# Grouped attention's projections run row by row beside the making of the modulated input; layer 1's last adaLN blocks beside its attention

## The chip, the cores and the metric

The kernel runs on one core of one Trainium2 chip. The metric is the device time of one execution in microseconds. The engines are called TensorE (PE in the rows; PEld is its weight load), the vector engine (DVE), the scalar engine (ACT), the Pool engine (POOL) and the sync engine (SP), whose queue issues most transfers.

## What is computed

Two layers of a hybrid backbone over 512 latent and 256 context tokens of width 1024, float32. Cut to what the change touches:

```python
for l in range(DEPTH):                                     # DEPTH = 2
    shift, scale, gate = split(silu(c) @ ada_w + ada_b, 3)  # adaLN; the context has its own vector
    pl = split_cols(modulate(x, shift, scale) @ in_w, IN_SPLITS)    # modulate: layer_norm(x) * (1 + scale) + shift
    ...
    q, k, v = gqa_project(pl[6], pl[7], pl[8], q_norm, k_norm, rope64)
    #   q: 4 heads of 64, k and v: 2 heads of 64; q and k: rms_norm, then rope (latent tokens only)
    oc = softmax_attention(q, k, v, GQA_SCALE)             # latent tokens read context and latent
    ...
    x = post_norm(ALPHA * x + gate * merge_branches(...), ln_g, ln_b)
```

The three other mixers (latent attention, RWKV-7, differential attention) and the merge follow the same input. In layer 1 the context's queries are not needed.

## The kernel before

**Tiles.** The 768 tokens are six tiles of 128 (0 and 1 context, 2 to 5 latent); the 1024 channels are eight blocks d of 128. Each float32 operand of a large product is split into a high and a low part, and three matmuls per tile and block are summed in PSUM (high by high, high by low, low by high). `w_split` (L280) loads a weight, copies the high part on the scalar engine (L292) and subtracts on the vector engine (L295).

**Start, layer 0** (`_run_layers`, L1525). The tokens are loaded and normalised. Then, for each of four adaLN blocks b, `ada` (L376) runs eight small float32 matmuls on c, which the trace counts as 16, with streamed weights (L391, `adaw`, twelve buffers), copies the row out (E, L396), turns it to columns (L399) and adds the bias (L403); after each block `make_xhat` (L454) is called for d = 2b and 2b+1. It transposes the six token tiles (L599, in `tok_T`), applies scale and shift while reading PSUM (L461 on the vector engine for context, L464 on the scalar engine for latent), and splits the result: for an even d on the vector engine (L478, L479), for an odd d on the scalar and Pool engines (L475, L476). PSUM has one pool A of eight one-bank buffers here.

**Projections of grouped attention.** The attention's pools are then opened, and `gq_proj` (L887) calls `m_stream` (L548): it loops over the eight channel blocks and, for each, over the token tiles, 144 matmuls of 256 columns in layer 0 (L570). Only after the last block it evicts Q tile by tile (L889), followed by the head norm (`head_rms`: squares L851, sums L852, reciprocal root L270 to L277), the scaling (L866, L867) and the rope (L590 to L593, with one multiplication on Pool, L592). `gkv_proj` (L870) does the same for K and V with 144 matmuls of 288 columns (L570), evictions L877 to L879. In layer 1 there are 96 and 144 matmuls, since Q is wanted for four tiles only.

**What sets the order.** The program is written as generators; the matmuls of other projections and of `ada` are `fill()`, advanced by rates `FILL` beside the attention's own steps (`beside`). A scheduler then puts the instructions of each engine in one fixed order. In layer 0, `fill()` also makes adaLN blocks 4 and 5 of layer 0 and blocks 0 to 3 of layer 1.

**Transition to layer 1** (L1662 on). The output projection, residual and post-norm run token by token (L1515, L1517, L432, L433), the second normalisation ends with L430. In a loop over d `make_xhat` runs for layer 1, with steps of `ada` for blocks 4 and 5 of layer 1 in between:

```python
more = K.ada(l + 1, ad, vec, xp, range(4, 6))
for _ in range(LEAD[0]):
    next(more)
for d in range(8):
    K.make_xhat(d, xn, ad, xp)
    for _ in range(LEAD[1]):
        next(more, None)
run(more)
```

## Time and profile before

| | |
|---|---|
| median of 3 runs | 2122.58 us (2116.28 to 2130.12) |
| the profiled execution, its own time | 2122.06 us |
| its span, first to last instruction | 2120.0 us |
| mean granted TensorE clock | 0.964 of full |
| busy: TensorE, its weight loads | 1932.8 us (91%), 1562.9 us (74%) |
| busy: vector, scalar, Pool engine | 1159.4 (55%), 816.2 (38%), 184.6 us (9%) |

The span is 2.06 us shorter than the execution's own time; the times in the rows count from the span's start. A granted clock of 1.00 is TensorE's full speed. In a timeline several instructions of one kind that follow each other stand in one row, with their count (x12) and the time from the first one's start to the last one's end; square brackets give the idle time ahead of it on its engine and what ended it. Layer 0's attention begins near 90 us, layer 1's near 1268 us.

### The profile page before, as it was taken

To read this page: it belongs to the slowest core of one execution; us is meant where nothing else is said; L and a number is where in the kernel's file an instruction comes from. 1 tells how busy PE (TensorE), PEld (TensorE's weight loads), DVE (VectorE), ACT (ScalarE), POOL (GpSimd) and SP (SyncE) were. 2 spreads that over 40 slices of the span, in tenths; PEclk is the share of its full clock that TensorE was granted. 3 is DMA by queue.
4 is the path that set the end of the run, shared out by engine and by line. 5 is a ranking of instruction groups with operands and counts; after the bars stand their busy time and mean duration, and the time that the engine had idled before them with its cause. 6 is when DMAs were issued, how large, how long until landed. Compare 5 with 4: busy or idle time off the path is not lost. (4 is left out here: it accounts for less than half of the span.)

```text
span 2120.0 us, 45780 instructions
## 1 busy us (share of the span) xinstructions
PE 1932.8 (91%) x19694; PEld 1562.9 (74%) x19694; DVE 1159.4 (55%) x2469; ACT 816.2 (38%) x1647; POOL 184.6 (9%) x283
## 2 busy tenths in 40 slices
...
GB/s 281 32 31 28 55 89 81 81 61 30 58 71 71 73 80 79 71 72 110 256 149 105 119 43 21 44 39 39 34 21 90 84 69 69 87 77 76 230 173 40
DMA packets 62322, 176.00 MB, mean 83 GB/s; under 512 B 7416, under 2 KB 12200, under 8 KB 62120
## 3 DMA queue, kind: packets, MB, share of 16 engines
...
q8 instruction: 155, 2.54, 0.5%
q14 instruction: 47, 0.39, 0.1%
...
## 5 line engine op out<-in xcount | busy, mean ns | idle before, releaser
L302 PE MATMUL ps<-xh,wx 128*128 128x384 f32 (+2 forms) x3096 | 690.5, 369 | 3.3 <-issue 1.9
L302 PEld LDWEIGHTS ps<-xh,wx 128*128 128x128 f32 x3096 | 535.1, 190 | 72.6 <-issue 16.0
L292 ACT ACTIVATE wx<-wx 128x1024 fp32r<-128x1024 f32 (+1 forms) x92 | 97.9, 1064 | 293.7 <-PE ps L302 224.4
L295 DVE TENSOR_TENSOR wx<-wx,wx 128x1024 fp32r<-128x1024 f32 (+1 forms) x92 | 113.4, 1232 | 129.4 <-ACT wx L292 126.5
L646 DVE TENSOR_REDUCE nmax<-ps 128x1 f32<-128x768 f32 (+1 forms) x160 | 134.7, 846 | 79.9 <-PE ps L643 78.6
L570 PE MATMUL ps<-wx,xh 128*128 128x256 f32 (+1 forms) x1200 | 156.1, 288 | 7.7 <-DVE mu L991 6.7
L570 PEld LDWEIGHTS ps<-wx,xh 128*128 128x128 f32 x1200 | 151.6, 191 | 10.6 <-ACT xc L475 6.8
L302 PE MATMUL ps<-xh,wb 128*128 128x384 f32 (+1 forms) x576 | 129.5, 375 | 26.5 <-DVE th L1473 17.9
L537 PE MATMUL ps<-wx,xh 128*128 128x256 f32 x960 | 141.3, 301 | 10.8 <-DVE oth L1407 5.8
L649 ACT ACTIVATE E<-ps,nmax 128x768 f32<-128x768 f32 (+1 forms) x160 | 130.1, 814 | 49.3 <-DVE nmax L646 44.7
L537 PEld LDWEIGHTS ps<-wx,xh 128*128 128x128 f32 x960 | 129.6, 203 | 18.5 <-DVE oth L1407 6.0
L643 PE MATMUL ps<-qk,qk 96*128 96x384 f32 (+3 forms) x504 | 131.2, 367 | 12.3 <-ACT E L649 11.8
L302 PEld LDWEIGHTS ps<-xh,wb 128*128 128x128 f32 x576 | 104.1, 195 | 48.4 <-DVE th L1473 15.5
L667 ACT ACTIVATE PH<-ps 128x512 f32<-128x512 f32 x156 | 91.7, 595 | 92.2 <-PE ps L665 89.4
L643 PEld LDWEIGHTS ps<-qk,qk 96*128 96x128 f32 (+1 forms) x504 | 82.6, 192 | 49.4 <-issue 22.6
L689 PE MATMUL ps<-PH,V 128*64 128x256 f32 x624 | 106.3, 414 | 3.2 <-ACT PH L667 2.8
L665 PE MATMUL ps<-cstalways,E 128*128 128x128 f32 x624 | 103.9, 288 | 5.1 <-DVE E L954 2.6
L1433 ACT ACTIVATE mth<-ps,hmb 128x384 f32<-128x384 f32 (+1 forms) x96 | 58.5, 610 | 118.5 <-PE ps L302 118.1
L665 PEld LDWEIGHTS ps<-cstalways,E 128*128 128x128 f32 x624 | 75.6, 146 | 26.5 <-issue 10.6
L625 DVE TENSOR_TENSOR qk<-ps,qk 32x256 fp32r<-32x256 f32 (+7 forms) x104 | 59.2, 574 | 36.9 <-ACT qk L624 34.7
L295 DVE TENSOR_TENSOR wx<-wf,wx 128x1024 fp32r<-128x1024 f32 (+2 forms) x34 | 41.1, 1210 | 59.8 <-PE ps L302 33.4
L624 ACT ACTIVATE qk<-ps 96x256 fp32r<-96x256 f32 (+3 forms) x104 | 51.2, 502 | 38.1 <-PE ps L599 37.5
...
## 6 DMA issues: line engine op xcount, KB each, us to landing
...
```

Source lines behind the costliest of these rows:

```text
L292: nc.scalar.activation(out=hi[:, :n], in_=raw[:, :n], func=AF.Copy)
L295: eng.tensor_tensor(out=lo[:, :n], in0=raw[:, :n], in1=hi[:, :n].bitcast(F32), op=ALU.subtract)
L302: self.nc.tensor.matmul(o, lhsT=w, rhs=x[:, s] if s is not None else x, start=first and p == 0, stop=last and p == 2)
L537: self.nc.tensor.matmul(ps[:, j * n:j * n + n], lhsT=self.xtok(x[k], s), rhs=w, start=k == 0 and p == 0 and j == 0, stop=k == 7 and p == 2 ...
L570: self.nc.tensor.matmul(ps, lhsT=self.xtok(x[k], s), rhs=w[:, c], start=k == 0 and p == 0 and head, stop=k == 7 and p == 2 and (tail or t ...
L625: nc.vector.tensor_tensor(out=lo[r, s], in0=ps[r], in1=hi[r, s].bitcast(F32), op=ALU.subtract)
L643: nc.tensor.matmul(o, lhsT=qt[:n, q], rhs=kt[:n, s], start=i == 0, stop=i == len(passes) - 1)
L646: nc.vector.tensor_reduce(out=nm, in_=v, axis=AX.X if ctx else AX.XY, op=ALU.max, negate=True)
L649: nc.scalar.activation(out=self.halves(e[:, :n], v), in_=v, func=AF.Exp, bias=nm, accum_out=den)
L665: nc.tensor.transpose(pt[:, c:c + 128], e[:, (k0 + k) * 128:(k0 + k) * 128 + 128], self.ident)
L667: nc.scalar.activation(out=hi, in_=pt, func=AF.Copy)
L689: nc.tensor.matmul(po[64 * (kk % 2):64 * (kk % 2) + 64, :n], lhsT=v2(kk), rhs=x[:, s], start=kk < 2, stop=kk >= nk - 2)
```

## The change

A generator `early_proj` takes over the first part of the projections of grouped attention. It opens six PSUM banks (pool G) at once: in layer 0 three hold Q for all six token tiles (two tiles a bank) and three hold K and V for three tiles; in layer 1 two hold Q for the four latent tiles and four hold K and V of four tiles. After each `make_xhat(d)` one row of the product, channel block d, is issued for all of these tiles: 27 matmuls in layer 0, 24 in layer 1. Weights are loaded for two rows at a time, Q's and KV's in one tile of 1088 columns (`wg`), split on the scalar and vector engines. The banks are evicted after the last row. The other tiles of K and V (three in layer 0, two in layer 1) follow in `m_stream`, which loads the K and V weights again. The pool for transposes and adaLN, A, has two banks beside the six; in layer 0's output projection too. The adaLN weights of the start get six buffers in place of twelve. Blocks 4 and 5 of layer 1's adaLN go from the transition to `fill()` of layer 1's attention, so both layers treat them alike. Line numbers after the change are higher by one up to L868 (L302 becomes L303), and L571 is the matmul of `m_stream`; L911 is the matmul of the rows.

```diff
--- before.py
+++ after.py
@@ -38,6 +38,7 @@
 QN = 256
 EB = 6
 QB = 8
+QSW, KSW = 384, 384
 GC = 2
 
 
@@ -866,29 +867,66 @@
         self.nc.vector.tensor_tensor(out=xv, in0=xv, in1=r, op=ALU.mult)
         eng.tensor_tensor(out=xv, in0=xv, in1=self.bc[g].unsqueeze(1).unsqueeze(1).to_broadcast(shape), op=ALU.mult)
 
+    def gqa_tiles(self):
+        self.gq = self.t(self.ap, [128, NT, QSW], "Qs", bufs=1)[:, :, :256]
+        self.gk = self.t(self.ap, [128, NT, KSW], "Ks", bufs=1)[:, :, :128]
+        self.gv = self.t(self.ap, [128, NT, 4, 64], "V2", bufs=1)[:, :, :2]
+        self.kr = self.t(self.ap, [128, NT, 32], "kr", bufs=1)
+
+    def use_q(self, t, o):
+        self.nc.scalar.activation(out=self.gq[:, t], in_=o, func=AF.Copy)
+
+    def use_kv(self, t, o):
+        self.nc.vector.tensor_copy(self.kr[:, t], o[:, 256:])
+        self.nc.scalar.activation(out=self.gk[:, t], in_=o[:, :128], func=AF.Copy)
+        self.nc.scalar.activation(out=self.gv[:, t], in_=o[:, 128:256].rearrange("p (h d) -> p h d", h=2), func=AF.Copy)
+
+    def early_proj(self, l, qt, pool):
+
+
+        nc = self.nc
+        self.gqa_tiles()
+        jobs = []
+        for i in range(0, len(qt), 2):
+            ps = self.P("G")
+            jobs += [(qt[i + j], ps[:, j * 256:j * 256 + 256], "gq", 0, 256, j == 0, j == 1, self.use_q) for j in range(2)]
+        early = range(6 - len(qt) // 2)
+        self.late = range(len(early), NT)
+        for t in early:
+            jobs.append((t, self.P("G")[:, :288], "gkv", 512, 288, True, True, self.use_kv))
+        off = _offsets()[0]
+        for k0 in range(0, 8, 2):
+            raw, hi, lo = (self.t(pool, [128, 1088], f"wg{x}", F32R if x else F32, bufs=2) for x in range(3))
+            for n, c, w in (("gq", 0, 256), ("gkv", 512, 288)):
+                o = off[n][0] + k0 * w
+                nc.sync.dma_start(out=raw[:, c:c + 2 * w], in_=self.a["inw"][l][:, o:o + 2 * w])
+            nc.scalar.activation(out=hi, in_=raw, func=AF.Copy)
+            nc.vector.tensor_tensor(out=lo, in0=raw, in1=hi.bitcast(F32), op=ALU.subtract)
+            for k in range(k0, k0 + 2):
+                for t, ps, n, c, w, head, tail, use in jobs:
+                    s = slice(t * 128, t * 128 + 128)
+                    c = slice(c + (k - k0) * w, c + (k - k0) * w + w)
+                    for p, (x, ww) in enumerate(((self.xh, hi), (self.xh, lo), (self.xl, hi))):
+
+                        nc.tensor.matmul(ps, lhsT=self.xtok(x[k], s), rhs=ww[:, c], start=k == 0 and p == 0 and head,
+                                         stop=k == 7 and p == 2 and tail)
+                yield
+        for t, ps, n, c, w, head, tail, use in jobs:
+            use(t, ps)
+
     def gkv_proj(self, l):
-        nc = self.nc
         toks = range(NT)
-        Ks = self.t(self.ap, [128, NT, 384], "Ks", bufs=1)[:, :, :128]
-        V2 = self.t(self.ap, [128, NT, 4, 64], "V2", bufs=1)[:, :, :2]
-        kr = self.t(self.ap, [128, NT, 32], "kr", bufs=1)
-
-        def use(t, o):
-            nc.vector.tensor_copy(kr[:, t], o[:, 256:])
-            nc.scalar.activation(out=Ks[:, t], in_=o[:, :128], func=AF.Copy)
-            nc.scalar.activation(out=V2[:, t], in_=o[:, 128:256].rearrange("p (h d) -> p h d", h=2), func=AF.Copy)
-        self.m_stream(l, "gkv", toks, use)
+        self.m_stream(l, "gkv", self.late, self.use_kv)
+        Ks = self.gk
         r = self.head_rms(Ks, 2, toks, 1.0, 1e-6)
-        self.scale_heads(Ks, 2, toks, r, "gkn", nc.vector)
+        self.scale_heads(Ks, 2, toks, r, "gkn", self.nc.vector)
         self.rope(Ks[:, NCT:].rearrange("p t (h d) -> p t h d", h=2), 2, 64)
-        return Ks, V2, kr
+        return Ks, self.gv, self.kr
 
     def gq_proj(self, l, qt):
-        nc = self.nc
-        Qs = self.t(self.ap, [128, NT, 384], "Qs", bufs=1)[:, :, :256]
-        self.m_stream(l, "gq", qt, lambda t, o: nc.scalar.activation(out=Qs[:, t], in_=o, func=AF.Copy))
+        Qs = self.gq
         r = self.head_rms(Qs, 4, qt, GQA_SCALE, 1e-6)
-        self.scale_heads(Qs, 4, qt, r, "gqn", nc.vector)
+        self.scale_heads(Qs, 4, qt, r, "gqn", self.nc.vector)
         self.rope(Qs[:, NCT:].rearrange("p t (h d) -> p t h d", h=4), 4, 64)
         return Qs
 
@@ -1528,7 +1566,9 @@
     ad = K.new_ada()
     xst, xct = ExitStack(), ExitStack()
     K.xp, K.xc = xst.enter_context(mk("xh0", 16)), None
-    with mk("xn0") as xp0, K.psum(A=(1, 8)):
+    ast = ExitStack()
+    K.ap = ast.enter_context(mk("at0"))
+    with mk("xn0") as xp0, K.psum(A=(1, 2), G=(1, 6)):
         xn = []
         for t in range(NT):
             x = K.t(xp0, [128, 1024], "xn", bufs=NT)
@@ -1537,9 +1577,13 @@
         K.normalise_all(xn, xp0)
         K.xh, K.xl = [], []
         for b in range(4):
-            run(K.ada(0, ad, vec, xp0, [b], (xp0, 12)))
+            run(K.ada(0, ad, vec, xp0, [b], (xp0, 6)))
+            if b == 0:
+                proj = K.early_proj(0, range(NT), xp0)
             for d in (2 * b, 2 * b + 1):
                 K.make_xhat(d, xn, ad, xp0)
+                next(proj)
+        run(proj)
     for l in range(DEPTH):
         last = l == DEPTH - 1
         qt = range(NCT, NT) if last else range(NT)
@@ -1553,8 +1597,7 @@
 
         def fill():
             yield from K.rwkv_inputs(l)
-            if l == 0:
-                yield from K.ada(0, ad, vec, K.ep, range(4, 6))
+            yield from K.ada(l, ad, vec, K.ep, range(4, 6))
             if not last:
                 nxt["vec"] = K.layer_vectors(l + 1)
                 nxt["ad"] = K.new_ada()
@@ -1564,8 +1607,7 @@
                     yield
                 yield from K.out_gate(l, i, O[i], qt, K.ep)
         ready = set()
-        with mk(f"qk{l}", QB) as K.qp, mk(f"ep{l}", EB) as K.ep, mk(f"at{l}") as K.ap, \
-                mk(f"wf{l}") as K.fp, K.psum(S=(2, 2), T=(1, 2), F=(1, 1), O=(1, 1)):
+        with mk(f"qk{l}", QB) as K.qp, mk(f"ep{l}", EB) as K.ep, mk(f"wf{l}") as K.fp, K.psum(S=(2, 2), T=(1, 2), F=(1, 1), O=(1, 1)):
             K.ps["A"] = K.ps["T"]
             K.load_group("rope", K.ap)
             K.load_rows(l, _BC_ATTN, K.ap)
@@ -1594,6 +1636,7 @@
         if only == "attn":
             return
         K.fp = None
+        ast.close()
         left = ExitStack()
         xct.close()
         K.rp = mkr(f"rw{l}")
@@ -1659,10 +1702,11 @@
                     next(tail)
                 gates_ = {s: K.gate_rows(ad, s) for s in ((1,) if last else (0, 1))}
                 run(tail)
-        with K.psum(A=(1, 8)):
+        with K.psum(**(dict(A=(1, 8)) if last else dict(A=(1, 2), G=(1, 6)))):
             ys = K.out_operands(y, len(qt) * 128)
             if not last:
-                ws = [K.out_weights(l, 0, mkr(f"ow0{l}"))]
+                ost = ExitStack()
+                ws = [K.out_weights(l, 0, ost.enter_context(tc.tile_pool(name=f"ow0{l}", bufs=1, side="right")))]
             left.close()
             xn = dict(h)
 
@@ -1678,20 +1722,20 @@
                 ws.append(K.out_weights(l, 1, owp))
                 K.out_proj(ys, ws, qt, gates_, h, first, second)
             if not last:
+                ost.close()
                 vec, ad = nxt["vec"], nxt["ad"]
                 K.xh, K.xl = [], []
                 xst.close()
                 K.xp = xst.enter_context(mk(f"xh{l + 1}", 16))
                 K.xc = xct.enter_context(mk(f"xc{l + 1}", 16)) if l + 1 == DEPTH - 1 else None
+                ast = ExitStack()
+                K.ap = ast.enter_context(mk(f"at{l + 1}"))
                 with mk(f"xn{l}") as xp:
-                    more = K.ada(l + 1, ad, vec, xp, range(4, 6))
-                    for _ in range(LEAD[0]):
-                        next(more)
+                    proj = K.early_proj(l + 1, range(NCT, NT), xp)
                     for d in range(8):
                         K.make_xhat(d, xn, ad, xp)
-                        for _ in range(LEAD[1]):
-                            next(more, None)
-                    run(more)
+                        next(proj)
+                    run(proj)
         right.close()
     xst.close()
 
```

How this moves instructions, at three places. First TensorE in layer 0, at the border of two adaLN blocks. Names: `xn` are normalised tokens (transposes), `adaw` adaLN weights, `wg` the new weights, `xh` the modulated input. Before:

```order
L599 MATMUL ps_298<-cstalways_113,xn_143 128x128
L391 MATMUL ps_308<-adaw_309,cs_118 32x512 x2
L391 MATMUL ps_308<-adaw_313,cs_118 32x512 x2
L391 MATMUL ps_308<-adaw_317,cs_118 32x512 x2
L391 MATMUL ps_308<-adaw_321,cs_118 32x512 x2
L399 MATMUL ps_327<-sum_46_121,E_325 128x2 x4
L599 MATMUL ps_337<-cstalways_113,xn_133 128x128
L599 MATMUL ps_337<-cstalways_113,xn_135 128x128
```

and now:

```order
L600 MATMUL ps_409<-cstalways_113,xn_145 128x128
L600 MATMUL ps_409<-cstalways_113,xn_147 128x128
L600 MATMUL ps_409<-cstalways_113,xn_149 128x128
L392 MATMUL ps_446<-adaw_447,cs_118 32x512 x2
L392 MATMUL ps_446<-adaw_451,cs_118 32x512 x2
L392 MATMUL ps_446<-adaw_455,cs_118 32x512
L911 MATMUL ps_245<-wg_107_371,xh_366 128x256
L911 MATMUL ps_245<-wg_108_372,xh_366 128x256
L911 MATMUL ps_246<-wg_107_371,xh_366 128x256
L911 MATMUL ps_245<-wg_107_371,xh_367 128x256
```

The last transposes of a pair of channel blocks (L599, now L600) were followed by the next adaLN block and its column turn (L399); now five of the eight adaLN matmuls stand there, then the 54 matmuls of two rows, and only then the other three.

Second, the vector engine in layer 0 between the modulated input's last channels and Q's head norm (`hm` holds the square sums, `kr` the part of K for latent attention, `mu` and what follows it are small constants). Before:

```order
L478 CAST xh_405<-mt_394 128x768
L479 TENSOR_TENSOR xh_406<-mt_394,xh_405 128x768
L295 TENSOR_TENSOR wx_540<-wx_538,wx_539 128x1024
L295 TENSOR_TENSOR wx_665<-wx_663,wx_664 128x1152
L852 TENSOR_REDUCE hm_622<-E_623 128x12
L852 TENSOR_REDUCE hm_622<-E_626 128x12
L295 TENSOR_TENSOR wx_743<-wx_741,wx_742 128x1152
L853 TENSOR_SCALAR hm_622<-hm_622 128x24
L270 TENSOR_SCALAR hr_630<-hm_622 128x24
```

and now:

```order
L880 COPY kr_244<-ps_248 128x32
L880 COPY kr_244<-ps_249 128x32
L880 COPY kr_244<-ps_250 128x32
L1029 TENSOR_TENSOR mu_184_909<-pp_111 128x8
L1032 TENSOR_SCALAR hw_185_912<-pp_111 128x4
L1033 TENSOR_SCALAR ha_186_913<-pp_111 128x4
L1030 TENSOR_SCALAR mu_184_909<-mu_184_909 128x8
L1034 TENSOR_SCALAR c_188_915<-pp_111 128x2
L1040 TENSOR_SCALAR nkk_922<-pp_111 128x2
L1035 TENSOR_SCALAR c_187_914<-c_188_915 128x2
L853 TENSOR_REDUCE hm_730<-E_731 128x12
L853 TENSOR_REDUCE hm_730<-E_734 128x12
```

Before, weight splits for the running projections (L295) stood ahead of Q's sums (L852); now the copies of the three early K and V tiles (L880) stand there, which come after the last row, and Q's sums (L853) behind them. In both kernels K's sums follow Q's whole chain.

Third, TensorE in the transition to layer 1 (`h` are normalised tokens). Before, at the end of the modulated input:

```order
L599 MATMUL ps_13176<-cstalways_113,h_1849_11549 128x128
L599 MATMUL ps_13176<-cstalways_113,h_1850_11551 128x128
L599 MATMUL ps_13176<-cstalways_113,h_1851_11553 128x128
L599 MATMUL ps_13176<-cstalways_113,h_1852_11555 128x128
L399 MATMUL ps_13200<-sum_46_121,E_13198 128x2 x4
L570 MATMUL ps_13245<-wx_13247,xh_13026 128x256
L570 MATMUL ps_13245<-wx_13248,xh_13026 128x256
L570 MATMUL ps_13245<-wx_13247,xh_13028 128x256
L570 MATMUL ps_13245<-wx_13247,xh_13026 128x256
```

and now, at its start:

```order
L600 MATMUL ps_13035<-cstalways_113,h_1860_11577 128x128
L600 MATMUL ps_13095<-cstalways_113,h_1860_11577 128x128
L600 MATMUL ps_13134<-cstalways_113,h_1855_11567 128x128
L600 MATMUL ps_13134<-cstalways_113,h_1856_11569 128x128
L911 MATMUL ps_13053<-wg_2164_13060,xh_13042 128x256
L911 MATMUL ps_13053<-wg_2165_13061,xh_13042 128x256
L911 MATMUL ps_13054<-wg_2164_13060,xh_13042 128x256
L911 MATMUL ps_13054<-wg_2165_13061,xh_13042 128x256
L911 MATMUL ps_13055<-wg_2164_13060,xc_13041 128x288
L911 MATMUL ps_13055<-wg_2165_13061,xc_13041 128x288
```

The first projection matmul stood behind the last of the 48 transposes and both adaLN turns (L399); the first row now follows the transposes of the first channel blocks.

## Rows read from the trace of the kernel before

**Rows 1.** Busy time by stretches: us, busy of each engine, granted clock, DMA share.

```profile
28.00:40.00 12.00, 10.48 (x89) 7.13 (x90) 6.87 (x21) 6.83 (x11) 3.62 (x2) 1.00 0.60 235
40.00:60.00 20.00, 19.02 (x156) 18.56 (x155) 5.81 (x7) 5.85 (x11) 2.63 (x1) 1.00 0.40 130
60.00:80.00 20.00, 20.00 (x154) 20.00 (x154) 16.05 (x33) 7.65 (x17) 2.72 (x5) 1.00 0.11 34
80.00:100.00 20.00, 11.75 (x62) 9.05 (x61) 12.88 (x33) 9.29 (x24) 1.52 (x2) 0.74 0.09 27
1200.00:1210.00 10.00, 4.65 (x24) 1.49 (x25) 7.91 (x39) 4.25 (x5) 0.00 (x0) 0.72 0.39 140
1210.00:1220.00 10.00, 5.76 (x29) 4.66 (x29) 9.18 (x13) 7.89 (x13) 5.76 (x8) 0.67 0.59 194
1220.00:1230.00 10.00, 6.87 (x38) 6.90 (x39) 5.20 (x17) 1.71 (x3) 1.97 (x2) 0.59 0.06 19
1520.00:1540.00 20.00, 16.57 (x110) 12.11 (x110) 19.23 (x34) 15.09 (x32) 0.00 (x0) 1.00 0.05 8
```

**Rows 2.** Timeline, layer 0, one adaLN block: start, us, engine, line, operation, [idle, releaser].

```profile
33.08 1.05 PE L399 MATMUL ps<-sum,E 128*128 128x2 f32 x8 [0.72 <-ACT E L396]
...
33.99 1.51 PE L599 MATMUL ps<-cstalways,xn 128*128 128x128 f32 x12
...
35.43 1.92 PE L391 MATMUL ps<-adaw,cs 128*32 128x512 f32 x16
...
36.34 0.96 DVE L479 TENSOR_TENSOR xh<-mt,xh 128x768 fp32r<-128x768 f32 x1
...
38.07 1.05 PE L399 MATMUL ps<-sum,E 128*128 128x2 f32 x8 [0.72 <-ACT E L396]
```

**Rows 3.** Timeline, layer 0, projections of Q, K and V.

```profile
41.43 36.99 PE L570 MATMUL ps<-wx,xh 128*128 128x256 f32 x288 [0.93 <-ACT mt L464]
...
58.60 1.77 ACT L889 ACTIVATE Qs<-ps 128x256 f32<-128x256 f32 x6 [2.77 <-PE ps L570]
...
66.97 1.76 DVE L866 TENSOR_TENSOR Qs<-Qs,hr 128x1536 f32<-128x1536 f32 x1
...
70.44 1.22 DVE L295 TENSOR_TENSOR wx<-wf,wx 128x1024 fp32r<-128x1024 f32 x1
...
74.29 2.37 DVE L593 TENSOR_TENSOR Qs<-Qs,E 128x512 f32<-128x512 f32 x2 [1.30 <-POOL Qs L592]
```

**Rows 4.** Timeline, layer 0, end of K's chain and the first attention matmuls.

```profile
81.36 0.55 DVE L852 TENSOR_REDUCE hm<-E 128x6 f32<-128x384 f32 x1 [1.16 <-ACT E L851]
...
87.92 1.26 DVE L593 TENSOR_TENSOR Ks<-Ks,E 128x256 f32<-128x256 f32 x2 [0.62 <-POOL Ks L592]
...
90.84 0.69 PE L599 MATMUL ps<-cstalways,E 128*128 128x128 f32 x2 [7.38 <-DVE qk L625]
```

**Rows 5.** Timeline, transition to layer 1.

```profile
1209.83 1.33 PE L599 MATMUL ps<-cstalways,h 128*128 128x128 f32 x5 [2.25 <-ACT h L430]
...
1211.90 0.42 DVE L478 CAST xh<-mt 128x512 fp32r<-128x512 f32 x1
...
1213.32 1.27 POOL L476 TENSOR_TENSOR xh<-mt,xh 128x512 fp32r<-128x512 f32 x1 [13.54 <-ACT xh L475]
1213.54 1.33 DVE L478 CAST xh<-mt 128x512 fp32r<-128x512 f32 x1
...
1223.13 14.01 PE L570 MATMUL ps<-wx,xh 128*128 128x256 f32 x96 [6.70 <-DVE mu L991]
```

**Rows 6.** Timeline, layer 1, head chains and the first attention matmuls.

```profile
1244.21 1.22 DVE L866 TENSOR_TENSOR Qs<-Qs,hr 128x1024 f32<-128x1024 f32 x1
...
1265.97 1.26 DVE L593 TENSOR_TENSOR Ks<-Ks,E 128x256 f32<-128x256 f32 x2 [0.61 <-POOL Ks L592]
...
1268.16 0.69 PE L599 MATMUL ps<-cstalways,E 128*128 128x128 f32 x2 [7.54 <-ACT E L614]
```

## Prediction

> **What bounds the kernel now.** I read the busy time by stretches first, at the two places that the change touches. In layer 0, TensorE is busy 19.02 and 20.00 us of 20 in two stretches and then 11.75 [rows 1]: there is almost nothing to fill while the modulated input is made and projected, and the hole comes after. In the transition to layer 1 the three stretches from 1200 to 1230 have 4.65, 5.76 and 6.87 of 10 busy, 12.7 us idle, at granted clocks of 0.72, 0.67 and 0.59 [rows 1]; a full clock is the 2.4 GHz level, and at the lower level, 1.2 GHz, a matmul takes twice as long. The timelines say what the holes are. In layer 0, one block of the input takes 4.99 us from one L399 to the next (33.08 to 38.07), with 0.72 us idle each, waiting for the copy E [rows 2]. With three of these and the 0.93 us ahead of the projection [rows 3] that is 3.1 us. The 288 projection matmuls then run without a gap, 36.99 us [rows 3]: the 144 for Q until the first Q eviction at 58.60 (17.17 us, 0.119 each), the other 144, for K and V, in 19.8 us (0.1375 each). The hole of 7.38 us ends at 90.84 [rows 4]. It is the vector engine's chain on K: square sums, reciprocal root, scaling and rope, last L593 at 87.92 + 1.26 = 89.18. In layer 1 the same hole is 7.54 us, behind an L593 that ends at 1267.23 [rows 6], and the projection before it starts 6.70 us late [rows 5]. What ends that wait is put down to a small vector instruction; going by the pools it is the turnover of PSUM, since all transposed tiles must have been read first.
>
> So what sets the time at both places is when the last Ks is ready. I work out how far that moves.
>
> **Layer 0.** Q's evictions, 58.60 on, and its chain, up to the L593 at 74.29 + 2.37 = 76.66, now run under the K and V matmuls [rows 3]. In the changed kernel all six banks close with the last row, so no Q can be evicted before the last row, and the vector engine's order has Q's chain wholly ahead of K's. Let R be the end of the last row. From the first Q eviction to L866 before were 8.37 us (58.60 to 66.97), and from there to the end of L593 9.69 [rows 3]; so Q is ready at R + 18.1. K's chain follows: two reductions (0.55 each), the weight split between them (1.22, as at 70.44), then 7.27 from the end of the last reduction (81.36 + 0.55) to the last L593's end [rows 4]: another 9.6, Ks at R + 27.7. The 72 late K and V matmuls (72 x 0.1375 = 9.9 us) wait for the last eviction. Behind them on TensorE stand 24 filler matmuls and then the transposes of Q, which wait longer anyway, so this costs nothing; but all of it can't cover the chain to its end.
>
> R: the moved matmuls are no filler, as the transposes and the adaLN matmuls already stand back to back. The lower bound is the old end of the projection, 41.43 + 36.99 = 78.42, less the 9.9 that come later: 68.5. What keeps R above it is that the rows wait for their own input. A pair of rows takes 36 x 0.119 + 18 x 0.1375 = 6.76 us. With two banks for transposes instead of eight, the second set of transposes waits for the reads of the first; five of the next block's eight adaLN matmuls stand ahead of the rows and end about 4.95 us after the block's start; the low part of the first channel, L479, is ready at 4.2 before (37.30 less 33.08 [rows 2]) and at about 5.95 now, as L461 of the second channel and the wait for a bank come ahead of it. The hi part alone lets the first row begin at about 5.7; 5.7 + 6.76 and the rest of the adaLN with its wait for E (0.72 each) make 13.9 us for a block, where 4.99 + 6.76 = 11.75 is the work. Another weight split (1.3) on the vector engine ahead of the hi part makes one block 14.75. The first block starts its rows at 25.4 and the second block starts at 36.2; then 13.9, 14.75 and 10.8 for the last, which has no next block in it: R = 75.6, Ks at 103.3, where it was 89.18: **+14.3**. Bounds: R at 68.5 gives +7; two more us of waits +17.
>
> **Layer 1.** Row 0 can begin about when the first modulated channel is there, 1212: L478 starts at 1211.90, after the transposes at 1209.83 that wait for the last token's h [rows 5]. The change takes a wx split and the adaLN adds out of that token's chain, but puts two new splits of 1088 columns into it, about 1.3 each (by the 1.22 for 1024 [rows 3]); I take these for even. The clock there is low, so the first two rows (24 matmuls each, mean 0.128) run partly at the lower level and end at about 1220. Three further pairs cost 48 x 0.128 = 6.16 of matmul, 1.5 of transposes (1.51 for 12 [rows 2]) and about 2 of waits for the weight splits and the Pool engine's low parts (1.27 each [rows 5]): 9.7 a pair, R = 1249.2. From R to Ks it is layer 0's 27.7 less the shorter Q passes (1.22 against 1.76 for each of two, [rows 3, 6]) and less 0.4 for the shorter sums: 26.2. Ks at 1275.4, where it was 1267.23: **+8.2**. What the change gains is the 6.70 us wait and most of the idle time of 1200 to 1223; what it gives up is again the cover of Q's chain, 15 us long. Bounds: rows without waits, R = 1242, +1; a us more of waits per pair, +12.
>
> **Layer 1's adaLN blocks.** Two blocks, 16 matmuls in 1.92 and 8 in 1.05 [rows 2], 5.9 us in all, go from the transition, where they stood in the shadow of the last token's normalisation, into the attention as filler. The slackest stretch there has 3.4 us idle in 20, with the vector engine busy 19.23 [rows 1], and the blocks bring eight weight loads and eight small vector adds with them. I take **+4**, between 0 (all of it in such gaps) and 6 (none).
>
> **At nothing:** the second load and split of the late weights; six instead of twelve buffers for adaLN weights (a pair of rows, 6.8 us, stands ahead of the use; without it a block would wait for a load); the new loads on SP's queue, which stand ahead of the late weights and of the filler's (the chain of 27.7 us covers these); and two banks in the output projection.
>
> Sum, on the profiled execution's 2122.06 (0.5 below the median, 2122.58): 2122.06 + 14.3 + 8.2 + 4 = **2148.6 us**.
>
> One thing in the rows speaks for the upper bounds. The hi copy L478 took 0.42 us alone and 1.33 beside a Pool subtraction (1211.90 and 1213.54, L476 at 1213.32) [rows 5]. The Trainium skill ("SBUF — State Buffer", "SBUF: two separate sides") has the vector engine and GpSimd share a port pair that one instruction locks for its whole length; this stretch agrees, with 0.9 us lost. If each of the three later layer 1 pairs lost that once more, the sum would be 2151.3.
>
> **Rivals.** (1) *The holes are filled and nothing is given back: faster.* Rows run inside the 12.7 us idle of the transition and the 3.1 of layer 0, so 2122.06 - 15.8 = 2106.3. It decides from the point where layer 1's last row ends before 1267.23 - 26.2 = 1241 and layer 0's before 61.5. For it: the idle time is there. Against it: layer 0's lower bound is 68.5, and Q's chain no longer runs under matmuls. (2) *Rows pack at the lower bound*: +7 + 1 + 0 = 2130.1. For it: the scheduler places adaLN matmuls between transposes and rows, so PE may not wait; against: the two banks. (3) *The clock falls between rows.* If layer 1's 192 early matmuls all ran at the lower level, 192 x 0.128 = 24.6 more than in the forecast: 2173. For it: the granted clock was 0.59 in 1220 to 1230 though L570 ran from 1223 [rows 1, 5]. Against it: with gaps of 0.72 every 5 us in layer 0 [rows 2] the granted clock was 1.00 from 28 to 40 [rows 1]. The Trainium skill ("TensorE: Matmul & The Clock Gate", "A second HAM failure mode: psum-queue depth-cycling") tells of a kernel whose clock swung because the engine idled briefly and often between groups while going through PSUM banks; by it the time would be near 2173, and layer 0's rows don't bear it out.
>
> **How the numbers follow.** Forecast 0.58, rival 1 0.08, rival 2 0.22, rival 3 0.12. A measurement of this kernel can tell about 1% from no change, so 2101 and 2143 are the marks. Faster by that: the better half of rival 1, which 2106.3 itself does not reach, 0.05. Same: the rest of it, rival 2, and the forecast's lower fifth, 0.36. Slower 0.59. The forecast's own range is 2138 to 2158; with rival 2 below it and the milder half of rival 3 the range is 2122 to 2163.
>
> **What would show it.** Right: layer 0's last row (L911) ends near 75.6 and layer 1's near 1249; the first late matmul (L571) waits for an eviction; Q's chain runs after the last row, K's behind it; the holes ahead of the first attention matmuls end near 105 and 1276, with the same work after them. Wrong: a layer 1 row stretch that ends before 1241, granted clocks near 0.5 in either row stretch, or an attention of layer 1 that is not longer by some us in spite of its two more blocks.

## The result, and the profile after

The changed kernel took 2178.8 us (median of four runs, 2169.6 to 2181.9), before beside it 2122.3: a ratio of 1.025, 95% interval 1.0225 to 1.0276. The forecast was 2148.6 and its range ended at 2163. The direction was right, the size was not: +56 us by the medians (53 by the ratio) where +26.5 was said. The profiled execution is the fastest of the four, 2169.6 us, with a span of 2167.4 against 2120.0; the 47.4 us between these spans can be placed, the 9 us from there to the median are in no profile.

The page of the changed kernel, busy times by engine:

```profile
PE 1949.5 (90%) x19694; PEld 1570.1 (72%) x19694; DVE 1165.0 (54%) x2473; ACT 823.1 (38%) x1651; POOL 179.8 (8%) x283
```

The work is the same, yet TensorE is busy 16.7 us longer, and 30.7 us more of the span are idle. Busy times by stretches of the changed kernel (columns as in [rows 1]; the first six answer to rows there, the last two lie behind layer 1's attention):

```profile
40.00:60.00 20.00, 16.60 (x111) 11.26 (x114) 7.73 (x17) 6.27 (x9) 1.81 (x1) 0.91 0.62 235
60.00:80.00 20.00, 18.19 (x126) 15.09 (x119) 7.17 (x12) 5.73 (x8) 3.79 (x2) 0.91 0.01 2
80.00:100.00 20.00, 15.11 (x116) 14.66 (x115) 16.07 (x40) 9.68 (x26) 3.02 (x8) 1.00 0.24 79
1200.00:1210.00 10.00, 7.46 (x36) 5.67 (x34) 9.16 (x31) 1.25 (x1) 0.00 (x0) 1.00 0.38 123
1210.00:1220.00 10.00, 0.25 (x2) 0.01 (x1) 7.55 (x28) 2.52 (x3) 1.47 (x1) 0.52 0.62 197
1220.00:1230.00 10.00, 5.02 (x20) 4.05 (x21) 6.48 (x22) 4.56 (x5) 1.65 (x1) 0.50 0.14 58
1230.00:1260.00 30.00, 27.95 (x211) 26.31 (x211) 11.24 (x26) 11.33 (x18) 7.92 (x9) 0.98 0.11 36
...
1620.00:1640.00 20.00, 15.00 (x98) 14.59 (x97) 8.51 (x21) 2.60 (x5) 5.29 (x5) 0.83 0.10 27
1640.00:1660.00 20.00, 14.31 (x94) 13.71 (x93) 4.14 (x6) 3.65 (x6) 3.29 (x6) 0.86 0.27 79
```

The two places of the forecast are slower as it said. But the last two stretches lie where it did not look: TensorE has 5.0 and 5.7 us of 20 idle, at clocks of 0.83 and 0.86. What stands there? First the end of layer 1's attention (the last L698 or L699), then the output gates' matmuls (L537 before, L538 after) up to RWKV's first L1245 or L1283. In TensorE's timeline of before:

```profile
1607.22 0.41 PE L698 MATMUL ps<-cstalways,E 128*128 128x128 f32 x2
...
1641.23 0.71 PE L1245 MATMUL ps<-cstalways,BK 64*128 64x64 f32 x16
```

and of the changed kernel:

```profile
1617.62 0.38 PE L699 MATMUL ps<-cstalways,E 128*128 128x128 f32 x2
1617.75 3.11 PE L538 MATMUL ps<-wx,xh 128*128 128x256 f32 x24
1623.40 7.51 PE L538 MATMUL ps<-wx,xh 128*128 128x256 f32 x48 [2.54 <-DVE E L1445]
1633.37 7.50 PE L538 MATMUL ps<-wx,xh 128*128 128x256 f32 x48 [2.46 <-DVE E L1445]
1642.74 10.38 PE L538 MATMUL ps<-wx,xh 128*128 128x256 f32 x72 [1.86 <-DVE E L1445]
...
1693.24 0.71 PE L1283 MATMUL ps<-cstalways,BK 64*128 64x64 f32 x16
```

Before, that stretch takes 34.0 us; after, 75.6. Most of the gates now run by themselves: TensorE is busy 59.3 of these 75.6 us, at a granted clock of 0.84 (28.4 of 34.0 before, at 0.90). Three of the groups shown wait 1.9 to 2.5 us for L1445, the vector instruction that reads a finished gate; groups further on wait for weight splits. The groups of the attention's own stretch (line, shape, count | busy us, mean ns | idle), of before, 1268.1 to 1607.4:

```profile
L537 PE MATMUL ps<-wx,xh 128*128 128x256 f32 x210 | 33.8, 300 | 0.1
```

and of the changed kernel, 1284.5 to 1617.7:

```profile
L392 PE MATMUL ps<-wf,cs 128*32 128x512 f32 x32 | 7.4, 607 | 0.3 <-DMA wf<-in_adaw_dram 0.3
...
L538 PE MATMUL ps<-wx,xh 128*128 128x256 f32 x24 | 4.5, 326 | 0.0
```

Of 384 gate matmuls, 210 lay inside the attention and 24 do now. The two adaLN blocks stand ahead of the gates in `fill()`, and `FILL`'s rates were left as they were: the attention takes 80 steps of filler, of which 74 had something to do before; now 92 are wanted.

The 47.4 us by stretches, each from the first matmul of attention (the L599 or L600 behind the hole) or the end of a phase:

| | before | after | longer by |
|---|---|---|---|
| start to layer 0's first attention matmul | 90.84 | 109.08 | 18.2 |
| from there to the output projection's end | 1102.3 | 1097.2 | -5.1 |
| transition to layer 1's first attention matmul | 75.1 | 78.4 | 3.3 |
| layer 1's attention | 339.1 | 333.0 | -6.1 |
| gates behind it | 34.0 | 75.6 | 41.6 |
| the rest | 478.8 | 474.2 | -4.6 |

Each figure is from one profiled execution. The second row need not be a gain: in the kernels below whose layer 0 is that of before this stretch is 1098.6 to 1111.8. The sum of the fourth and fifth rows is far steadier: 373.1 before, and 371.1 to 373.3 in the five kernels below in which that part was left as it was.

### The profile page after: what moved, and what is told of

It is laid out like the page before. It is cut to its first block, busy times and chain, and to the rows that moved or that the text cites. A ratio compares the mean times of both kernels' runs of the same rounds, so it can differ in the third digit from the quotient of the medians.

```text
span 2167.4 us, 45817 instructions
## 1 busy us (share of the span) xinstructions
PE 1949.5 (90%) x19694; PEld 1570.1 (72%) x19694; DVE 1165.0 (54%) x2473; ACT 823.1 (38%) x1651; POOL 179.8 (8%) x283
## 5 line engine op out<-in xcount | busy, mean ns | idle before, releaser
L303 PE MATMUL ps<-xh,wx 128*128 128x384 f32 (+2 forms) x3096 | 693.6, 370 | 1.7 <-issue 1.0
L303 PEld LDWEIGHTS ps<-xh,wx 128*128 128x128 f32 x3096 | 537.5, 190 | 71.7 <-issue 15.1
L538 PE MATMUL ps<-wx,xh 128*128 128x256 f32 x960 | 144.1, 311 | 24.6 <-ACT wx L293 8.9
L538 PEld LDWEIGHTS ps<-wx,xh 128*128 128x128 f32 x960 | 135.0, 214 | 31.4 <-ACT wx L293 9.7
L303 PE MATMUL ps<-xh,wb 128*128 128x384 f32 (+1 forms) x576 | 125.9, 368 | 26.9 <-DVE th L1511 19.3
L303 PEld LDWEIGHTS ps<-xh,wb 128*128 128x128 f32 x576 | 102.3, 191 | 47.2 <-DVE th L1511 16.1
L571 PE MATMUL ps<-wx,xh 128*128 128x256 f32 (+1 forms) x840 | 107.3, 285 | 2.7 <-ACT V L882 2.7
L571 PEld LDWEIGHTS ps<-wx,xh 128*128 128x128 f32 x840 | 104.0, 188 | 5.3 <-ACT V L882 3.2
L600 PE MATMUL ps<-cstalways,E 128*96 128x128 f32 (+1 forms) x240 | 41.9, 298 | 27.7 <-ACT E L615 16.7
```

What stands on the lines that cost most here:

```text
L303: self.nc.tensor.matmul(o, lhsT=w, rhs=x[:, s] if s is not None else x, start=first and p == 0, stop=last and p == 2)
L538: self.nc.tensor.matmul(ps[:, j * n:j * n + n], lhsT=self.xtok(x[k], s), rhs=w, start=k == 0 and p == 0 and j == 0, stop=k == 7 and p == 2 ...
L571: self.nc.tensor.matmul(ps, lhsT=self.xtok(x[k], s), rhs=w[:, c], start=k == 0 and p == 0 and head, stop=k == 7 and p == 2 and (tail or t ...
```

## The experiments

Kernels run beside the kernel before on one chip; "ratio" is against that. The expectations use these names. D: the adaLN blocks displace the gates from layer 1's attention. P: they cost their own work, as predicted. R: the rows cause the loss. W: the adaLN weight loads. S: the later start of the first adaLN block. C: Q's chain, no longer under matmuls, is what makes the rows slow. K: the rows' own waits. Attention and gates in the tables are worked out as in the last table.

**1. The adaLN move alone, and the change without it.** On the kernel before:

```diff
 def fill():
     yield from K.rwkv_inputs(l)
-    if l == 0:
-        yield from K.ada(0, ad, vec, K.ep, range(4, 6))
+    yield from K.ada(l, ad, vec, K.ep, range(4, 6))
 ...
-more = K.ada(l + 1, ad, vec, xp, range(4, 6))
```

(all steps of `more` go too). And on the changed kernel the reverse, with the two blocks ahead of layer 1's rows:

```diff
-            yield from K.ada(l, ad, vec, K.ep, range(4, 6))
+            if l == 0:
+                yield from K.ada(0, ad, vec, K.ep, range(4, 6))
 ...
+                    run(K.ada(l + 1, ad, vec, xp, range(4, 6)))
                     proj = K.early_proj(l + 1, range(NCT, NT), xp)
```

> The kernel before with one part of the change only: blocks 4 and 5 of layer 1's adaLN go from the transition into the filler of layer 1's attention. Theory D (displacement): their 18 filler steps push the output gates' projections (the last filler) out of the attention, 12 steps are left when it ends, and these run alone afterwards; in the changed kernel the end of these projections moved by 36 us against the start of the attention. So this kernel should be 25 to 36 us slower than before, and the first projection ahead of it earlier by 0 to 7. Rival P (price of the work alone, as predicted): +0 to +6 us. Rival R (the 36 us come from the rows, by a late start of weights and a cold clock, not from the adaLN): within 3 us of before.

> The changed kernel with blocks 4 and 5 of layer 1's adaLN back in the transition, ahead of the first row; all else of the change stays. Theory D: the attention of layer 1 and the gates behind it go back to their old length, some 36 us less than the changed kernel, while the transition pays up to 6: 2140 to 2152 us by the median, 13 us of layer 0 and 3 to 9 of the transition over before. Rival P: at most 6 us less than the changed kernel, so 2170 or more. Rival R: no difference to the changed kernel.

The move alone: 2146.1, ratio 1.0097 (1.0076 to 1.0118), 21 us. Without it: 2153.2, ratio 1.0132 (1.0095 to 1.0168), so it is worth 25 us of the whole change (1.025 less 1.0132). Both are less than D expected (25 to 36, and some 36), but far more than P and R allow. In the profiles the move alone makes attention and gates 34.5 us longer and the transition 6.1 shorter; this alone is the largest part of the loss.

**2. Layer 0's rows alone.** The changed kernel with layer 1 as before (`early_proj`, its banks and the adaLN move undone there).

> Rows by the side of the modulated input in layer 0 alone; the transition to layer 1, its projections and its adaLN blocks as before. From the trace of the changed kernel the first attention matmul of layer 0 came 18.2 us later than before and the end of the output projection 13.1 us: 11 to 15 us slower than before. The prediction's term said +14.3. Rival (the layer 0 delay is absorbed by a slack of layer 1): less than 5 us.

2144.7, ratio 1.0082 (1.0053 to 1.011), so 17.4 us, above the 11 to 15 expected. Layer 1's rows, with the two blocks in the transition, are then 1.0132 less 1.0082, 10.6 us.

**3. Is it the displacement or the work?** The filler's rates for layer 1 raised in the changed kernel; the same in the kernel before; and in the kernel before lowered, so that about as many gates as in the change fall behind, with no adaLN moved:

```diff
-FILL = ((0.7, 0.65, 0.9), (0.5, 0.4, 0.5))
+FILL = ((0.7, 0.65, 0.9), (0.6, 0.5, 0.6))     fill_rates (on after), rates_alone (on before)
+FILL = ((0.7, 0.65, 0.9), (0.4, 0.33, 0.35))   gates_behind (on before)
```

> The changed kernel with the filler's rates in layer 1's attention raised from 0.5, 0.4 and 0.5 to 0.6, 0.5 and 0.6, so that 97 instead of 80 steps are taken beside the attention, where 92 are there. Theory D: no gate projection is left behind the attention; 20 to 33 us less than the changed kernel. Rival W (the eight added weight loads through two buffers are what is paid, not the place of the gates): less than 8 us faster. Rival R: no difference.

> The kernel before with the filler's rates in layer 1's attention lowered from 0.5, 0.4 and 0.5 to 0.4, 0.33 and 0.35: 61 of 74 filler steps are taken beside the attention, 13 are left when it ends, as 12 are in the changed kernel; no adaLN work is moved. It prices the pushed-out gates by themselves. Theory D: from the first attention matmul of layer 1 to the end of the gate projections 8 to 15 us longer than before's 373.1, since raising the rates in the changed kernel gave 9.9 back. If the pushed-out gates were all of the 34.5 us of the move alone, it would be 25 or more; if they were nothing, under 3.

> The kernel before with the filler's rates in layer 1's attention raised to 0.6, 0.5 and 0.6 and nothing else: no adaLN block is moved, so the fillers run out earlier in the attention. From the first attention matmul of layer 1 to the end of the gates, 373.1 before. If the raised rates themselves cost what is left of the 25.7 us (half of the matmuls taken away gave 5.8 back, so all of them about 12): 385 to 390. If they cost nothing and the steps are what is paid: 370 to 376.

| | attention | gates | sum | gate matmuls inside | ratio (95%) |
|---|---|---|---|---|---|
| before | 339.1 | 34.0 | 373.1 | 210 | |
| after | 333.0 | 75.6 | 408.6 | 24 | 1.025 (1.0225 to 1.0276) |
| move alone | 332.3 | 75.3 | 407.6 | 24 | 1.0097 (1.0076 to 1.0118) |
| gates_behind | 324.5 | 73.1 | 397.6 | 32 | 1.0079 (1.0051 to 1.0107) |
| fill_rates | 360.4 | 38.3 | 398.8 | 196 | 1.0193 (1.0167 to 1.0219) |
| rates_alone | 359.2 | 33.8 | 392.9 | 209 | 1.0086 (1.0056 to 1.0115) |

gates_behind, groups of its attention, 1273.1 to 1597.7:

```profile
L537 PE MATMUL ps<-wx,xh 128*128 128x256 f32 x32 | 5.5, 303 | 0.0
```

This shows the displacement: with no adaLN moved, the sum grows by 24.5 us, more than the 8 to 15 that D expected. By the ratio the whole kernel is 17 us longer (11 to 23); behind the gates 4.3 us come back (474.5 where it was 478.8), as in the change. The 178 gate matmuls that left the attention are 28.7 us of work (33.8 / 210 each); inside, they had cost only 14.6 (339.1 less 324.5), behind it they cost 39.1. Added to it is the adaLN work itself, 7.4 (L392) and 2.1 (L400's sixteen): 24.5 + 9.5 = 34.0, against 34.5 for the move alone. That the sum fits is no proof of its parts: the lower rates also thin out the filler that stays, and busy time is not the price of work inside the attention (experiment 4 puts the blocks lower).

That higher rates would cure it was wrong. They bring 196 of the gates back, but the attention grows by 27 us, and the sum is still 25.7 above before. Rates raised with nothing moved cost 19.9 by themselves (18 by the ratio). The stretches of rates_alone at the end of the attention:

```profile
1580.00:1600.00 20.00, 15.82 (x91) 11.25 (x89) 15.30 (x27) 13.98 (x29) 2.37 (x2) 0.80 0.18 54
1600.00:1620.00 20.00, 16.86 (x84) 9.51 (x83) 16.25 (x30) 13.82 (x30) 0.00 (x0) 0.84 0.00 1
1620.00:1640.00 20.00, 19.39 (x96) 11.76 (x95) 10.13 (x23) 10.27 (x21) 0.00 (x0) 0.68 0.00 0
```

The filler is used up early and the transfers stop (0.00); what is left of the attention runs alone, at clocks of 0.80, 0.84 and 0.68. Before, the five stretches from 1500 to 1600 held 110 to 139 matmuls in 20 us each, here 84 to 96. So the rates of before lie between two losses of this stretch, 24.5 and 19.9 us.

**4. Is it the adaLN weights or matmuls, or how they are mixed?** On the kernel before with the move and raised rates, each block keeps one of its four weight loads and all matmuls, or all loads and half of its matmuls, in one step (what is left out stands in the expectations). Then nothing left out, but fewer and larger steps, each with two loads and four matmuls into the four column groups; for all of layer 1's blocks that are filler, or for blocks 4 and 5 alone:

```diff
+w2 = [...]                      # two loads a step
+for k in range(4):
+    i = 2 * q + k
+    nc.tensor.matmul(ps[32 * (i % 4):32 * (i % 4) + 32], lhsT=self.cc[:, 2 * i:2 * i + 32],
+                     rhs=w2[k // 2][:, k % 2 * 512:k % 2 * 512 + 512], start=i < 4, stop=i >= 4)
```

> The move alone with rates 0.6, 0.5 and 0.6, and one weight load in place of four for each of the two adaLN blocks in layer 1's attention: all matmuls of a block read the first load, so the gates of layer 1 are computed from wrong adaLN columns; steps and matmuls stay. First attention matmul of layer 1 to the end of the gates: with all loads 398.8 (with the changed kernel's rows). If the loads are what is paid: 375 to 383. If the matmuls or the raised rates: 393 to 401.

> The same rates, all eight loads and all steps, but of each block's eight matmuls only four are made, all from the first load in one group (the gates of layer 1 are computed from part of the sum). The same stretch: if the matmuls are what is paid, 5 to 10 us less than 398.8. If the loads or the raised rates: 395 or more.

> The kernel before with layer 1's adaLN blocks 4 and 5 in its attention, as in the move alone (+22 us), but with two weight loads per filler step, so that eight matmuls stand together and 10 steps come in place of 18, and the last rate 0.6, so that no gate projection is left behind the attention. Theory D with its two parts (pushed-out gates, and matmuls of 0.5 us each where 16 together took 1.92): the attention and gates are 6 to 14 us longer than before instead of 34.5, the transition 6 shorter as in the move alone: 2122 to 2132 by the median of before's 2124. Rival W (the eight weight loads through two buffers are what is paid): no better than the move alone with raised rates, +10 or more.

> The move alone with two weight loads per filler step for these two blocks only (in the run with pairs layer 0's filler was changed too, and its end came 11.6 us later), and rates 0.55, 0.45 and 0.6, so that 91 steps are there for 84. Layer 0 as before. From the first attention matmul of layer 1 to the end of the gates: theory D 380 to 391 us (373.1 before, 407.6 in the move alone, 398.8 with raised rates), and 2122 to 2136 by the median. Rival W: 395 or more.

One load: 2137.6 in a single run, attention and gates 393.4. Half the matmuls: 2136.3 in a single run, 393.0. That is as long as with the raised rates and no adaLN at all (392.9), and 5 to 6 us less than with all of it (398.8). The 398.8 is from a kernel with the changed rows, which make this stretch 1 to 2 us longer (408.6 and 407.6 above, 375.4 and 373.3 below). So beyond the rates, the two blocks cost some 4 to 6 us, and it can't be said whether loads or matmuls. Larger steps for all blocks: 2142.2, ratio 1.0086 (1.0062 to 1.011), sum 391.3 with rates of 0.5, 0.4 and 0.6. For blocks 4 and 5 alone, with 0.55, 0.45 and 0.6: 2142.5, ratio 1.0078 (1.0055 to 1.0102), sum 398.1 although 213 gate matmuls stood inside. Both missed what D expected (2122 to 2132; a sum of 380 to 391). In the second the blocks' own matmuls count 12.6 us and wait 2.6 for their loads:

```profile
L389 PE MATMUL ps<-wf,cs 128*32 128x512 f32 x32 | 12.6, 765 | 2.6 <-DMA wf<-in_adaw_dram 2.6
```

So the loads can cost something too, as W said, but not most of it. No rate or mix that was tried brings the sum near 373 with the blocks in layer 1's attention.

**5. The blocks elsewhere.** Layer 0's filler has 171 steps in the attention, 25 of them without work. With the blocks put there, on the kernel before and on the changed one:

```diff
-                yield from K.ada(l + 1, nxt["ad"], nxt["vec"], K.ep, range(4))
+                yield from K.ada(l + 1, nxt["ad"], nxt["vec"], K.ep, range(6))
```

> The kernel before with blocks 4 and 5 of layer 1's adaLN in the filler of layer 0's attention, behind blocks 0 to 3, where 25 of 171 steps found nothing left to do; the transition has none of them. Theory D (what costs is a filler without room): 18 steps fit into the 25, so layer 0 grows by no more than 2 to 8 us and the transition shrinks by 6: 2118 to 2127 where before has 2124. Rival W (the blocks cost 18 us or more beside any attention): 2136 or more.

> The changed kernel with blocks 4 and 5 of layer 1's adaLN in layer 0's filler, where 25 steps found nothing to do, in place of layer 1's attention. Theory D: the stretch from the first attention matmul of layer 1 to the end of the gates is 373 us again (408.6 in the changed kernel) and the transition stays near 78.4; the kernel is 25 to 35 us faster than the changed one, 2143 to 2154. Rival (the rows themselves spoil layer 1's attention): the stretch stays over 390.

On the kernel before: 2122.5, ratio 0.9994 (0.9977 to 1.0011), attention and gates 373.3, transition 70.0. On the changed kernel: 2152.7, ratio 1.0123 (1.0097 to 1.0149), 375.4. In place of the 25 us that they cost in layer 1's full filler, the blocks cost no more here, where the filler had room, than they did in the transition. There they were not in a shadow: it is 5 to 6 us shorter without them. This gain doesn't show in the whole (-1.3 us, interval -5 to +2), so the blocks may cost some of it in layer 0: the first kernel's output projection ends at 1198.2, 5 us later than before, but that is within the spread of the kernels with an unchanged layer 0 (1190.9 to 1204.5).

**6. The start.** In the changed kernel `at0` opens ahead of the tokens' loads, and the scheduler puts its rope and norm-row loads there; the first adaLN matmul comes at 16.18 instead of 14.12. With these in a pool of their own, opened with the attention:

```diff
-            K.load_group("rope", K.ap)
-            K.load_rows(l, _BC_ATTN, K.ap)
+            K.load_group("rope", cnp)
+            K.load_rows(l, _BC_ATTN, cnp)
```

> The changed kernel, but the rope table and the norm rows of the attention are taken from a pool that opens with the attention, so that their two loads can't move to the start, where they stand on the scalar engine's queue beside the tokens' loads. In the changed kernel the first adaLN matmul came at 16.2 us, before at 14.1. Theory S: these two loads cost the start 2 us, the first adaLN matmul comes at 14 to 14.5 and the kernel is 1.5 to 2.5 us faster than the changed one (a difference that only the profile can show, not the median). Rival: the start is late because the weights of the rows share the queue; no difference at the start.

The first adaLN matmul is back at 14.09, but the first attention matmul comes at 110.5 (109.1 with the change): ratio 1.0269 (1.0236 to 1.0301). The second pair of rows still begins 2.0 us earlier than in the change (44.77 for 46.79), the third later (62.52 for 61.68): from 56 to 64 the granted clock is 0.57 here and was 1.00 there. So the 2 us are real up to that point and then covered by the clock; whether they would count in the end stays open. They are not what makes layer 0 18 us late.

**7. Rows for Q alone.** On the kernel before, only Q in rows, in two banks (three in layer 0), evicted ahead of the K and V matmuls, which stay as they were; A has six banks (five in layer 0). In layer 1, in both layers, and in layer 1 with the blocks in layer 0's filler:

```diff
+    def early_q(self, l, qt, pool):     # the row loop of early_proj, Q's banks and weights alone
 ...
     K.make_xhat(d, xn, ad, xp)
+    next(proj)
```

> The kernel before with rows beside the modulated input for Q alone and in layer 1 alone (two open banks, six for transposes); K and V wholly in the later stream, adaLN in the transition. Theory C (what costs the change its gain is that Q's chain has lost its cover): with K and V's 144 matmuls still behind the rows, Q's chain lies under them, and the idle 12.7 us of the transition hold rows: the first attention matmul of layer 1 comes 5 to 10 us earlier after the output projection than before's 75.1, and the kernel is 4 to 10 us faster. Rival K (rows beside the modulated input lose by their own waits and the clock, whatever is behind them): the span from the output projection to the attention is not shorter than 75.

> The same in both layers: in layer 0 three open banks for Q's rows, five for transposes and adaLN, K and V wholly behind. Theory C: Q's chain is under the K and V stream again, so layer 0 costs only what the rows' own waits are, 0 to 6 us at its first attention matmul, against 15 to 21 in the changed kernel. Rival K: 10 us or more there.

> Both together: Q's rows beside layer 1's modulated input, K and V behind, and the two adaLN blocks in layer 0's filler. Theory C: the transition, 72.4 with the rows for Q alone and 69.0 without the adaLN blocks, comes to 64 to 68 us where before has 75.1; with 2 to 8 us more in layer 0 the kernel is 2 to 9 us faster than before. Rival: the transition is bound by the last token's normalisation and the chain on K, so that the two gains are the same one: 69 or more.

Layer 1: 2119.7, ratio 0.9981 (0.9963 to 0.9999), transition 72.4 where it was 75.1. Both: 2127.5, ratio 1.0022 (1.0004 to 1.0041), layer 0's first attention matmul at 93.90, 3 us late, not 18 (in kernels with an unchanged layer 0 it comes at 88.8 to 92.8). With the blocks moved as well the transition is 67.7, but the ratio 1.0005 (0.9988 to 1.0022): no faster, where 2 to 9 us were expected. C fits layer 0: with Q's chain under K's and V's matmuls and five banks, most of the 18 us is gone. The two causes were changed together there, so their shares stay open. In layer 1 the gain is 2.7 us in the transition, half of the least that was expected, and in the whole 0.2%; it is the only kernel whose interval ends below 1.

TensorE's timeline of q_early_both, one block of layer 0:

```profile
42.80 1.05 PE L399 MATMUL ps<-sum,E 128*128 128x2 f32 x8 [0.71 <-ACT E L396]
43.71 1.51 PE L599 MATMUL ps<-cstalways,xn 128*128 128x128 f32 x12
45.15 1.90 PE L391 MATMUL ps<-adaw,cs 128*32 128x512 f32 x10
46.98 4.49 PE L904 MATMUL ps<-wg,xh 128*128 128x256 f32 x36
```

## Why the prediction was wrong, step by step

**The step that failed: layer 1's adaLN blocks, +4 (0 to 6).** By the timed ratios the three terms were:

| term | forecast | measured |
|---|---|---|
| layer 0 | +14.3 | +17.4 (experiment 2) |
| layer 1's rows, blocks in the transition | +8.2 | +10.6 (experiments 1, 2) |
| adaLN blocks, what the transition gains included | +4 | +25.0 (after less experiment 1) |

The sum of these is 53. The first is good to some 6 us; the others are differences with two intervals in each, good to some 10. 21 of the 26.5 us by which 53 exceeds the forecast are the third term. The forecast weighed the 5.9 us of matmuls against the gaps of one stretch [rows 1], and never asked what stood behind them: `fill()` is one queue, so every step put in at its head pushes another out at its end. What was pushed out cost 24.5 by itself (experiment 3): 178 gate matmuls, 28.7 us of work, took 14.6 us inside the attention and 39.1 behind it. The second error was smaller and in the other direction: the blocks did not stand "in the shadow" in the transition, which is about 6 us shorter without them.

**Layer 0, +14.3: right in kind, its parts off.** The end of the rows and of Ks in the changed kernel:

```profile
79.81 2.65 PE L911 MATMUL ps<-wg,xh 128*128 128x256 f32 x20
79.90 2.06 ACT L877 ACTIVATE Qs<-ps 128x256 f32<-128x256 f32 x6 [3.66 <-PE ps L911]
83.90 1.33 PE L571 MATMUL ps<-wx,xh 128*128 128x288 f32 x8 [1.43 <-ACT V L882]
...
106.15 1.27 DVE L594 TENSOR_TENSOR Ks<-Ks,E 128x256 f32<-128x256 f32 x2 [0.62 <-POOL Ks L593]
...
109.08 0.69 PE L600 MATMUL ps<-cstalways,E 128*128 128x128 f32 x2 [6.34 <-DVE qk L626]
```

R is 82.46, 6.9 later than forecast; Ks is ready at 107.42, 18.2 later than before (14.1 by the forecast's own Ks, 103.3 less 89.18) and outside the +17 of the bounds. It comes 24.96 behind R where 27.7 were forecast: the last row has Q's matmuls ahead of K's and V's, so Q's eviction begins at 79.90, 2.56 ahead of R, and the forecast counted it from R. An error of 6.9 and one of 2.7 the other way are in the +14.3, so that it came near is in part luck. Where R was lost is seen in the first and the last rows and in two blocks between them:

```profile
27.61 9.24 PE L911 MATMUL ps<-wg,xh 128*128 128x256 f32 x54
...
39.45 1.05 PE L400 MATMUL ps<-sum,E 128*128 128x2 f32 x8 [0.74 <-ACT E L397]
...
41.19 0.89 PE L600 MATMUL ps<-cstalways,xn 128*128 128x128 f32 x6 [0.42 <-DVE ada L404]
42.72 0.77 PE L600 MATMUL ps<-cstalways,xn 128*128 128x128 f32 x4 [0.64 <-DVE mt L462]
43.42 3.44 PE L392 MATMUL ps<-adaw,cs 128*32 128x512 f32 x10
46.79 6.91 PE L911 MATMUL ps<-wg,xh 128*128 128x256 f32 x54
...
55.40 1.05 PE L400 MATMUL ps<-sum,E 128*128 128x2 f32 x8 [0.71 <-ACT E L397]
...
59.26 0.66 PE L600 MATMUL ps<-cstalways,xn 128*128 128x128 f32 x4 [1.22 <-DVE mt L462]
59.84 1.90 PE L392 MATMUL ps<-adaw,cs 128*32 128x512 f32 x10
...
73.61 0.93 PE L600 MATMUL ps<-cstalways,xn 128*128 128x128 f32 x4 [0.69 <-ACT mt L465]
74.21 8.26 PE L911 MATMUL ps<-wg,xh 128*128 128x256 f32 x54
```

A block takes 15.95 us (39.45 to 55.40; 14.75 and 13.9 forecast). The rows themselves, 54 matmuls in 6.91, are the 6.76 of the forecast, except for the first, 9.24, and the last, 8.26. The transposes wait for readers of the two banks, as it said, but in this block the clock goes down behind them, which it reckoned with in layer 1 alone. Busy times of the part of each block that is no row, and of pieces of the first rows, of the ten adaLN matmuls and of the last rows:

```profile
28.00:30.00 2.00, 2.00 (x11) 2.00 (x10) 0.71 (x1) 1.97 (x3) 0.27 (x1) 0.50 0.98 372
...
39.40:46.80 7.40, 6.30 (x31) 2.70 (x31) 4.22 (x9) 3.39 (x4) 1.54 (x1) 0.77 0.77 286
43.40:45.40 2.00, 2.00 (x10) 0.56 (x10) 1.89 (x3) 1.62 (x2) 0.14 (x1) 0.50 0.56 229
...
55.40:61.70 6.30, 4.67 (x31) 2.54 (x31) 5.17 (x10) 4.49 (x6) 0.02 (x1) 1.00 0.01 3
...
74.00:76.00 2.00, 2.00 (x11) 1.93 (x10) 1.11 (x2) 1.39 (x2) 0.00 (x0) 0.50 0.00 0
```

The same 31 matmuls take 7.40 and 6.30 us. In the first, after waits of 0.74, 0.42 and 0.64, the granted clock is 0.77, with 0.50 (the lower level, 1.2 GHz) in 43.4 to 45.4, and ten adaLN matmuls take 3.44; in the second, in spite of waits of 0.71, 0.42 and 1.22, it is 1.00 (2.4 GHz) and they take 1.90. It is 0.50 too in the first rows, which take 2.33 us longer than the others, and behind a wait of 0.69 in the last, which take 1.35 longer. So the clock may go to its lower level beside waits as short as these, and need not. The first of the two stretches has transfers beside it (0.77) and the second none (0.01), but the last rows slow down without any (0.00). The lower clock is thus 2.33 + 1.54 + 1.35 = 5.2 of the 6.9 us, and 2.1 are the later start (experiment 6); the rest was 0.4 shorter than forecast. This is what the term had wrong: it took the full clock throughout. The five other kernels with these rows in layer 0 have R from 79.59 (ada_back) to 85.56 (early_layer0), and each has a stretch of 4 us at 0.50 to 0.57 between 40 and 80: how much the clock takes differs among these profiles.

**Layer 1's rows, +8.2: the rows cost that, the step that it was worked out from did not.** With the blocks out of the transition in both, it is 69.0 us (move alone) and 78.4 (after): +9.4; in the other pair, 70.0 and 78.5, +8.5. But the forecast went from a Ks in a transition that holds the blocks (1267.23) to one in a transition that doesn't (1275.4), and that step is 75.1 to 78.4, +3.3: the blocks' leaving gave back 5 to 6 us that it had at nothing. So the agreement of 8.2 with the rows' price is luck. In the profile:

```profile
1212.44 1.11 ACT L903 ACTIVATE wg<-wg 128x1088 fp32r<-128x1088 f32 x1 [8.11 <-DMA wg<-in_inw_dram]
1213.58 1.29 DVE L904 TENSOR_TENSOR wg<-wg,wg 128x1088 fp32r<-128x1088 f32 x1 [2.45 <-ACT wg L903]
...
1221.66 0.69 PE L600 MATMUL ps<-cstalways,h 128*128 128x128 f32 x2 [11.41 <-ACT h L431]
...
1261.95 6.63 PE L571 MATMUL ps<-wx,xh 128*128 128x288 f32 x48 [1.29 <-ACT V L882]
...
1282.41 1.27 DVE L594 TENSOR_TENSOR Ks<-Ks,E 128x256 f32<-128x256 f32 x2 [0.62 <-POOL Ks L593]
...
1284.61 0.69 PE L600 MATMUL ps<-cstalways,E 128*128 128x128 f32 x2 [6.83 <-ACT E L615]
```

The weight splits do stand in the last token's chain, ahead of the h that TensorE waits 11.41 us for; they were taken as even with what left it. Counted from the output projection's end (1206.24, 13.1 later than before) the last row ends at +54.4 (56.1 forecast), and Ks comes 23.0 behind that (26.2 forecast); Q's eviction begins ahead of the row's end here too, at 1258.39. The hole before the attention is 6.83 [rows 6: 7.54], as said.

**The rivals.** The first (faster) and second (packed rows) fell: R is 82.46, not 68.5. The third came out in part. Most of layer 1's rows run at 0.98 (1230 to 1260), but the first run at 0.50, the sign that the forecast named, from 1226.82 to 1230. The low clocks of 1210 to 1230, 0.52 and 0.50, come in and behind the wait of 11.41; before, they were 0.67 and 0.59 [rows 1]. The clock falls in layer 0 too, for 5.2 us where the rival had 24.6 in layer 1. The Trainium skill ("TensorE: Matmul & The Clock Gate", "A second HAM failure mode: psum-queue depth-cycling") tells of a clock that swung with brief idling between groups as PSUM banks turned over; with two banks and a clock of 0.77 this trace agrees in the first block shown, and with 0.50 in the last rows; with 1.00 it does not in the second block.

**At nothing.** The late matmuls wait 1.43 and 1.29 us and run under the chain, as said. The late start, 2 us, was not named.

**Left open.** How layer 0's loss divides between Q's chain and the two banks; what lets the clock fall at one block border and not at another; the 9 us between after's profiled execution and its median; and whether some other set of rates would hold both adaLN blocks and gates.
